# A setup generator in a stream of its own, its rotation tables last and queued behind the decay masks, and a recurrence with two working steps per chunk

## The chip, the cores and the metric

The kernel runs on one core of a Trainium2 chip. The metric is device time in microseconds (us) for one execution, the median of three runs. The engines are called by the profile's names: PE (TensorE matmul; PEld its weight loads), DVE (VectorE), ACT (ScalarE), POOL (GpSimd), SP (SyncE, which here only issues DMAs).

## The reference, cut to what matters

One layer of a decoder trunk over 2048 rows of width 1024: a mixer, cross-attention into 256 memory rows, and a gated MLP. The change lies in the mixer, which has two groups of heads side by side:

```
proj = rmsnorm(x) @ w_in
y_s5  = s5_mixer(proj[:, :256], lam, dt, b, c, ...)          # diagonal group
y_ssd = ssd_mixer(z, xbc, dt_raw, conv_w, a_log, ...)        # 12 heads, chunks of 128 rows
x = x + concat([y_s5, y_ssd]) @ w_out

# s5: h[l] = a * h[l-1] + (B u[l]), a complex, 64 states in each of 16 groups; y = Re(C h) + d*u
# ssd, per chunk c and head h:
#   lmat = exp(where(causal, acs[l] - acs[s], -inf));  cb = C_c B_c^T
#   y_diag = (cb * lmat) @ (x*dt);  y_off = (C_c @ prev) * exp(acs)
#   prev = prev * exp(acs_last) + B_c^T @ (decay * x * dt)
```

The parameters of the diagonal group are turned into matrices that don't depend on the rows: `ww` (input to state), `cct` (state to output, and the direct term) and `tab`, cosines and sines of the phase at 256 positions for each of 16 groups (the rotation tables).

## The kernel before, in words

The mixer's input projection is done by `MixerIn.run`: four blocks of 512 rows, in each 22 projections of 128 columns. One projection is 24 matmuls of 128x512 in two halves of 12 (L123 to L125, the three products of a split of each operand into a high and a low part, L98 and L99). After each half `Kit.step()` takes one step of each of two lists of generators, so that their instructions lie between the matmuls of the projections:

- `fg`: `ssd`, the recurrence over the four chunks of a block, for one half (`pr`) of the heads at a time. It runs during the next ten or twelve projections. Its parts for a chunk are `stage_in` (transposes of x and B, L415 and L421), `stage_cb` (the product C B^T at L430, times the decays at L434), `stage_y` (L443 to L458) and `stage_out` (L466 to L470). The decays themselves are `fetch_L`, on POOL's queue: a DMA that spreads a row of `acs` over 128 partitions (L387) and an `affine_select` that masks it (L388), then six exponentials on ACT (`decay`, L403). The rows of `acs` come from `dtprep`: a copy on DVE (L371), then a DMA on POOL's queue (L372).
- `bg`: `norm1_rest`, which normalizes the rows of the later blocks (sum of squares on ACT, L136; the scale on DVE, L130; the power -0.5 on POOL, L131; the product on DVE, L139; transposes on PE, L148), 60 steps long, and behind it `s5_setup`. Short generators are put ahead of these as they arise: `ssq`, and `mem.prep()`, the norm of the memory rows, in the last block.

`s5_setup` is 112 steps long: small DVE instructions (sine and cosine, powers), then the rotation tables on POOL (40 steps: eight of small products, L639 to L644, and two per group of three 128x256 instructions each, L654 to L660, with a DMA to DRAM per group, L661), then for each quarter of the groups four combinations of three 128x512 DVE instructions each (L725 to L727), with matmuls (L743, L744), transposes (L768) and DMAs on POOL's queue (L731). The tables are made in the SBUF tiles `b1`, `b2`, `Ca`, `Cb` and `Ba`, into which the later part loads its parameters (L705, on SP's queue) and writes its results.

There are two steps per projection and one at the start of each later block. What is left of `bg` when the projections are done is drained in one go (`k.drain(bg=True)`), ahead of the key and value projections of the cross-attention, `mem.proj`.

The order on each engine's queue isn't that of the program text. It is fixed when the kernel is built, by the framework's scheduler: the program order gives each instruction its priority, and on an engine that its own cost model sees idle the scheduler issues the first by priority whose inputs it takes to be ready. So instructions that are written late can run early: the first memsets of the tables (L633), written at about the 65th step, start at 0.95 us. On the chip each queue then runs strictly in this order, whether the inputs are late or not.

Of the kernel before, what the change touches and what calls it, by code (L numbers as in the profile page):

```python
# [9 lines left out]
F32 = mybir.dt.float32  # L10
# [3 lines left out]
ALU = mybir.AluOpType  # L14
AX = mybir.AxisListType
P = 128
# [8 lines left out]
def bcol(a, n):  # L25

    return a.rearrange("p (a b) -> p a b", b=1).to_broadcast([a.shape[0], a.shape[1], n])


class Kit:  # L30


    def __init__(self, tc, cx):
        self.tc, self.nc = tc, tc.nc
        self.V, self.S, self.G, self.TE = tc.nc.vector, tc.nc.scalar, tc.nc.gpsimd, tc.nc.tensor
        ep = cx.enter_context
        self.cp = ep(tc.tile_pool(name="const", bufs=1))
        self.dp = ep(tc.tile_pool(name="dram", bufs=1, space=bass.MemoryType.DRAM))
        self.pp = ep(tc.tile_pool(name="ps", bufs=8, space=bass.MemoryType.PSUM))
        self.sm = ep(tc.tile_pool(name="small", bufs=4))  # L40
        self.fg, self.bg = [], []
        nc = self.nc
        self.ident = self.cp.tile([P, P], F32, name="ident")
        make_identity(nc, self.ident)
        self.m05 = self.cp.tile([P, 1], F32, name="m05")
        nc.vector.memset(self.m05, -0.5)
        self.gains = self.cp.tile([P, 32], F32, name="gains")
# [26 lines left out]


    def step(self, n=1, m=1):
        for lst, k in ((self.fg, n), (self.bg, m)):
            for _ in range(k):
                while lst:
                    try:  # L80
                        next(lst[0])
                        break
                    except StopIteration:
                        lst.pop(0)

    def drain(self, bg=False):
        lst = self.bg if bg else self.fg
        while lst:
            try:
                next(lst[0])  # L90
            except StopIteration:
                lst.pop(0)


    def halves(self, src, hi, lo, scale=None):
# [78 lines left out]
class MixerIn:  # L174
# [208 lines left out]
    def fetch_L(self, b, pr, c):  # L383

        L = self.Ls[:, self.nL % 4]
        self.nL += 1
        self.k.G.dma_start(out=L.rearrange("p h l -> p (h l)"), in_=flat(self.d["acs"][b, c:c + 1, pr * 6:pr * 6 + 6, :]).partition_broadcast(P))  # L387
        self.k.G.affine_select(out=L, in_=L, pattern=[[0, 6], [1, P]], compare_op=ALU.is_ge, fill=-1e30, base=0, channel_multiplier=-1)  # L388
        self.L[b, pr, c] = L

    def ssd(self, b, pr, dd, xs, Bs, Cs, zs, sqacc):
# [69 lines left out]
        def stage_out(c):  # L461
# [5 lines left out]
            for i in range(3):  # L467
                j = pr * 3 + i
                V.scalar_tensor_tensor(gt[i][:, cs], xs[i][:, cs], self.D[:, j:j + 1], py[:, i * 128:i * 128 + 128], op0=ALU.mult, op1=ALU.add)
                V.tensor_tensor(gt[i][:, cs], gt[i][:, cs], zs[j][:, cs], op=ALU.mult)  # L470
        stage_in(0)
        yield
        for c in range(4):
            stage_cb(c)
            n = pr * 4 + c + 3
            if n < 8:
                self.fetch_L(b, n // 4, n % 4)
            if c < 3:
                decay(c + 1)
            yield  # L480
            if c < 3:
                stage_in(c + 1)
                yield
            stage_y(c)
            yield
            if c:
                stage_out(c - 1)
                yield
        stage_out(3)
        yield  # L490
        for i in range(3):
# [20 lines left out]
        k.rstd(self.d["rs"][:, b * 4:b * 4 + 4], pq[:, 0:4], 0.25 / 768, 1e-6)  # L512
        yield

    def run(self, last):
        k = self.k
        hs = self.hs
        k.bg.insert(0, self.norm1_rest())
        for b in range(self.NB):
            if b:  # L520
                with k.tc.high_priority(400):
                    hs = [k.split(*raw, tag="h") for raw in hraw]
                    hs += [k.split(*raw, tag="h") for raw in self.fetch_h(b, range(4, 8))]
                k.step(2)
            sqacc = self.zp.tile([P, 512], F32, tag="sqa", name="sqa", bufs=2)
            zs = [None] * 6
            dtp = self.dtprep(hs, b)
            for i in range(2):
                p = self.proj(hs, i)
                ut = k.t()  # L530
                k.S.activation(ut, p, AF.Copy)
                k.nc.scalar.dma_start(out=self.d["u"][i][:, b * 512:b * 512 + 512], in_=ut)
                next(dtp, None)
            for pr in range(2):
                for i in range(3):
                    if b == self.NB - 1 and pr == 0 and i == 2:
                        k.bg.insert(0, last)
                    zs[pr * 3 + i] = self.zgate(self.proj(hs, 2 + pr * 3 + i), pr * 3 + i)
                    next(dtp, None)
                xs = []  # L540
                for i in range(3):
                    xs.append(self.conv(self.proj(hs, 8 + pr * 3 + i), pr * 3 + i))
                    next(dtp, None)
                Bs, Cs = [], []
                for i in range(2):
                    Bs.append(self.conv(self.proj(hs, 14 + pr * 2 + i), 6 + pr * 2 + i))
                    if pr == 1 and i == 1 and b + 1 < self.NB:
                        hraw = self.fetch_h(b + 1, range(4))
                    Cs.append(self.conv(self.proj(hs, 18 + pr * 2 + i), 10 + pr * 2 + i))
                k.drain()  # L550
                k.fg.append(self.ssd(b, pr, self.dd, xs, Bs, Cs, zs, sqacc))


def s5_setup(k, a, d, up, NJ):
# [71 lines left out]
        if q % 4 == 3:  # L626
            yield
    yield
    tw = sp.tile([P, 16, 8], F32, tag="tw", name="tw")
    few = []  # L630
    for n, q0 in (("B", 3), ("A", 7)):
        fc, fs = (sp.tile([P, 16, 16], F32, tag="5" + x, name="f" + x) for x in (("b1", "b2") if n == "B" else ("Ca", "Cb")))
        G.memset(fc[:, :, 0:1], 1.0)  # L633
        G.memset(fs[:, :, 0:1], 0.0)
        for q in range(4 if n == "B" else nst - 4):
            m = 1 << q
            er, ei, t = bcol(Er[:, q0 + q, :], m), bcol(Ei[:, q0 + q, :], m), tw[:, :, 0:m]
            co, so, ci, si = fc[:, :, m:2 * m], fs[:, :, m:2 * m], fc[:, :, 0:m], fs[:, :, 0:m]
            G.tensor_tensor(co, ci, er, op=ALU.mult)  # L639
            G.tensor_tensor(t, si, ei, op=ALU.mult)  # L640
            G.tensor_tensor(co, co, t, op=ALU.subtract)
            G.tensor_tensor(so, ci, ei, op=ALU.mult)
            G.tensor_tensor(t, si, er, op=ALU.mult)
            G.tensor_tensor(so, so, t, op=ALU.add)  # L644
            yield
        few.append((fc, fs))
    (cb, sb), (ca, sa) = few
    na = NJ // 16
    for g in range(16):
        tab = sp.tile([P, 2, na, 16], F32, tag="tab", name="tab", bufs=2)  # L650
        wk = sp.tile([P, 16, 16], F32, tag="5Ba", name="wk")[:, 0:na]
        a_ = lambda v: v[:, g, 0:na].rearrange("p (a b) -> p a b", b=1).to_broadcast([P, na, 16])
        b_ = lambda v: v[:, g, :].rearrange("p (a b) -> p a b", a=1).to_broadcast([P, na, 16])
        G.tensor_tensor(tab[:, 0], a_(ca), b_(cb), op=ALU.mult)  # L654
        G.tensor_tensor(wk, a_(sa), b_(sb), op=ALU.mult)
        G.tensor_tensor(tab[:, 0], tab[:, 0], wk, op=ALU.subtract)
        yield
        G.tensor_tensor(tab[:, 1], a_(sa), b_(cb), op=ALU.mult)
        G.tensor_tensor(wk, a_(ca), b_(sb), op=ALU.mult)
        G.tensor_tensor(tab[:, 1], tab[:, 1], wk, op=ALU.add)  # L660
        G.dma_start(out=d["tab"][g], in_=tab.rearrange("p h a b -> p h (a b)"))  # L661
        yield

    Xr, Xi, Yr, Yi = (sp.tile([P, 16, 9], F32, tag=n, name=n) for n in ("Xr", "Xi", "Yr", "Yi"))
    V.memset(Xr[:, :, 0:1], 1.0)
# [66 lines left out]
    for q in range(4):  # L732
# [26 lines left out]
        for w in range(2):  # L759
            if w == 0:  # L760
                WT = comb(gs, Ba, Yr[:, gs, 0:8], Bb, Yi[:, gs, 0:8], ALU.add)
            else:
                WT = comb(gs, Ba, Yi[:, gs, 0:8], Bb, Yr[:, gs, 0:8], ALU.subtract)
            for _ in range(4):
                yield
            p = k.ps()
            for i in range(4):
                TE.transpose(p[:, i * 128:i * 128 + 128], WT[:, i * 128:i * 128 + 128], k.ident)  # L768
            Ws = k.t()
            S.activation(Ws, p, AF.Copy)  # L770
            put(d["ww"][gs, :, w * 128:w * 128 + 128], Ws)
            yield


def stage_s5(k, a, d, T):
# [748 lines left out]
def trunk(tc, a, out, T):  # L1524
    with ExitStack() as cx:
# [8 lines left out]
        with ExitStack() as c1:  # L1534
            k.open(c1, 3, r=8, w=8, h=16, t=25)
            mem = Memory(k, a, d)
            with ExitStack() as c2:
                d["s5p"] = c2.enter_context(tc.tile_pool(name="s5p", bufs=1))
                mix = MixerIn(k, c2, a, d, T)
                k.bg.append(s5_setup(k, a, d, mix.u, NJ))  # L1540
                mix.run(mem.prep())
                k.drain(bg=True)
                K, Vt = mem.proj("wk", "wv"), mem.proj("wv", None)
                k.drain()
                k.drain(bg=True)
# [51 lines left out]
```

## Time and profile before

| | us |
|---|---|
| median of 3 runs | 2741.43 (2739.88 to 2743.27) |
| the profiled execution, its own time | 2741.57 |
| its span, first to last instruction | 2739.9 |
| PE busy | 2625.9 (96%) |
| DVE busy | 2136.0 (78%) |
| ACT busy | 1324.6 (48%) |
| POOL busy | 482.3 (18%) |
| mean granted PE clock | 0.983 |

The mixer's projections fill the span from about 15 to 728 us. In the profile's lists a group of instructions has its line, engine, operation, output tile and input tiles, and its count; then busy time and the mean duration in ns. In a list of waits, "PE ps L148 <- DVE raw L139" says that PE's instruction of line 148 that writes `ps` stood waiting for DVE's instruction of line 139 that writes `raw`; then come total us, times, and the longest. A row of stretches gives for each engine the busy time and the count in that stretch, then the granted PE clock, the busy share of the DMA engines and GB/s. In a timeline, the time in brackets is how long the engine was idle just before, and what ended it.

### The profile page before, as it was taken

How to read it: one execution, taken by the hardware profiler on the slowest of the kernel's cores; microseconds unless marked ns; L12 is line 12 of the kernel's file. 1: busy time of each engine (PE TensorE's matmuls, PEld its weight loads, DVE VectorE, ACT ScalarE, POOL GpSimd, SP SyncE). 2: the span in 40 equal slices, each digit the busy share in tenths (PEclk: the TensorE clock that was granted, in tenths of full speed). 3: DMA queues.
4: the chain of work that ended last, by engine and by line, in shares of the span. 5: the costliest groups of instructions: out<-in, count | busy, mean ns of one | idle time of the engine just before them, and what ended most of it. 6: DMA issues, size and time to landing. Idle time of an engine off the chain costs nothing. (4 is left out here: it accounts for less than half of the span.)

```text
span 2739.9 us, 38565 instructions
## 1 busy us (share of the span) xinstructions
PE 2625.9 (96%) x12636; PEld 2187.3 (80%) x12636; DVE 2136.0 (78%) x4015; ACT 1324.6 (48%) x2657; POOL 482.3 (18%) x807
## 2 busy tenths in 40 slices
PE   8479999999799999999999999999999999999997
PEld 6367888878699788888888888887888888788876
DVE  8568888888877654878789788879887887677776
ACT  4345654446445412778745454435444344433333
POOL 3840101101103110110311222212111111000000
PEclk9789999999899999999999999999999999999999
DMA  5445443344368783546665433425222227887886
GB/s 171 131 145 176 151 129 112 110 137 141 106 201 293 259 290 141 184 162 231 215 219 174 127 112 120 131 89 177 93 85 78 92 63 255 280 295 237 257 263 203
DMA packets 241538, 468.24 MB, mean 171 GB/s; under 512 B 30008, under 2 KB 72056, under 8 KB 241336
## 3 DMA queue, kind: packets, MB, share of 16 engines
q1 hardware_dynamic: 182312, 341.38, 38.1%
q0 software_dynamic: 30416, 105.50, 11.9%
q10 hardware_dynamic: 28608, 18.88, 2.2%
q8 instruction: 100, 1.64, 0.2%
q14 instruction: 102, 0.84, 0.1%
HBM read 350.67 MB, written 114.39 MB: 170 GB/s over the span
## 5 line engine op out<-in xcount | busy, mean ns | idle before, releaser
L124 PE MATMUL ps<-H,W 128*128 128x512 f32 x952 | 370.6, 389 | 0.5 <-DVE H L99 0.5
L123 PE MATMUL ps<-H,W 128*128 128x512 f32 x952 | 370.9, 390 | 0.0
L125 PE MATMUL ps<-H,W 128*128 128x512 f32 x952 | 370.5, 389 | 0.1
L123 PE MATMUL ps<-h,w 128*128 128x512 f32 (+1 forms) x736 | 301.8, 410 | 13.4 <-ACT w L98 10.5
L125 PE MATMUL ps<-h,w 128*128 128x512 f32 (+1 forms) x736 | 288.9, 392 | 0.5 <-DVE w L99 0.5
L124 PE MATMUL ps<-h,w 128*128 128x512 f32 (+1 forms) x736 | 287.6, 391 | 0.7 <-DVE h L102 0.7
L123 PE MATMUL ps<-Q,A 128*128 128x512 f32 x704 | 275.9, 392 | 1.0 <-ACT A L98 0.8
L125 PE MATMUL ps<-Q,A 128*128 128x512 f32 x704 | 274.5, 390 | 0.0
L124 PE MATMUL ps<-Q,A 128*128 128x512 f32 x704 | 273.9, 389 | 0.0
L98 ACT ACTIVATE W<-S 128x512 fp32r<-128x512 f32 x191 | 118.9, 630 | 283.2 <-DVE S L1350 143.5
L98 ACT ACTIVATE w<-r 128x512 fp32r<-128x512 f32 x224 | 139.1, 627 | 187.9 <-PE ps L124 143.6
L124 PEld LDWEIGHTS ps<-H,W 128*128 128x128 f32 x952 | 178.7, 188 | 38.2 <-DVE H L99 1.5
L125 PEld LDWEIGHTS ps<-H,W 128*128 128x128 f32 x952 | 178.7, 188 | 37.6 <-DVE W L99 0.5
L123 PEld LDWEIGHTS ps<-H,W 128*128 128x128 f32 x952 | 178.7, 188 | 37.4 <-ACT H L98 0.4
L99 DVE TENSOR_TENSOR w<-r,w 128x512 fp32r<-128x512 f32 x224 | 159.8, 717 | 62.2 <-ACT w L98 59.1
L123 PEld LDWEIGHTS ps<-h,w 128*128 128x128 f32 x736 | 140.8, 191 | 38.8 <-ACT w L98 10.9
L125 PEld LDWEIGHTS ps<-h,w 128*128 128x128 f32 x736 | 140.1, 190 | 31.3 <-DVE w L99 1.6
L124 PEld LDWEIGHTS ps<-h,w 128*128 128x128 f32 x736 | 141.0, 192 | 27.0 <-DVE h L102 2.1
L125 PEld LDWEIGHTS ps<-Q,A 128*128 128x128 f32 x704 | 132.1, 188 | 28.7 <-DVE A L99 1.1
L123 PEld LDWEIGHTS ps<-Q,A 128*128 128x128 f32 x704 | 132.2, 188 | 28.2 <-ACT A L98 1.0
L124 PEld LDWEIGHTS ps<-Q,A 128*128 128x128 f32 x704 | 132.3, 188 | 26.8
L98 ACT ACTIVATE A<-F 128x512 fp32r<-128x512 f32 (+1 forms) x146 | 89.0, 631 | 123.4 <-PE ps L124 63.9
(489 smaller groups left out, 6299.6 us busy)
## 6 DMA issues: line engine op xcount, KB each, us to landing
A<-actd SPq DMA_DIRECT2D x192, 256.0 KB, 3.9
r<-in_w_in SPq DMA_DIRECT2D x176, 256.0 KB, 2.9
R<-in_w_up SPq DMA_DIRECT2D x176, 256.0 KB, 2.9
R<-in_w_down SPq DMA_DIRECT2D x132, 256.0 KB, 4.3
actd<-U POOLq DMA_DIRECT2D x88, 256.0 KB, 3.1
A<-actd SPq DMA_DIRECT2D x96, 192.0 KB, 3.8
R<-h3Cd SPq DMA_DIRECT2D x56, 256.0 KB, 3.6
L<-acsd POOLq DMA_DIRECT2D x32, 384.0 KB, 4.3
```

The lines of the kernel that those rows point to most:

```text
L98: self.S.activation(hi, src, AF.Copy)
L99: self.V.tensor_tensor(lo, src, hi.bitcast(F32), op=ALU.subtract)
L123: self.TE.matmul(out, lh, rh, start=first and i == 0, stop=False)
L124: self.TE.matmul(out, lh, rl, start=False, stop=False)
L125: self.TE.matmul(out, ll, rh, start=False, stop=last and i == n - 1)
```

## The change

1. `s5_setup` leaves `bg` and becomes the only generator of a third list, `xg`, of which `step` also takes one step each time. It is put there at the start of the second half (`pr == 1`) of the first block, at the 25th step, while `norm1_rest` is still running in `bg`.
2. The rotation tables move from the middle of `s5_setup` to its end, after the last quarter. They take 56 steps there in place of 40 (an empty step in each group).
3. The first table instructions of each piece are traced under `behind()`, which orders them on POOL's queue after `k.mark`, the most recently traced mask (L388). The rest of a piece follows them by its data.
4. In `ssd`, `stage_in`, `stage_cb`, the next mask and the next decays are one step (`head`), with `stage_out` of the chunk before; `stage_y` is another; two empty steps lie between. The generator has 20 steps in place of 18.

```
     def step(self, n=1, m=1):
-        for lst, k in ((self.fg, n), (self.bg, m)):
+        for lst, k in ((self.fg, n), (self.bg, m), (self.xg, m)):
...
+    def behind(self):
+        return self.tc.issue_after(self.mark.ins)
...
-        self.k.G.affine_select(out=L, in_=L, ...)
+        self.k.mark = self.k.G.affine_select(out=L, in_=L, ...)
...
-        stage_in(0)
-        yield
-        for c in range(4):
+        def head(c):
+            stage_in(c)
             stage_cb(c)
             n = pr * 4 + c + 3
             if n < 8:
                 self.fetch_L(b, n // 4, n % 4)
             if c < 3:
                 decay(c + 1)
+        head(0)
+        yield
+        for c in range(4):
+            yield
+            stage_y(c)
+            yield
             yield
             if c < 3:
-                stage_in(c + 1)
-                yield
-            stage_y(c)
-            yield
+                head(c + 1)
             if c:
                 stage_out(c - 1)
-                yield
+            yield
...
             for pr in range(2):
+                if b == 0 and pr == 1:
+                    k.xg.append(beside)
...
     # s5_setup: the tables, from after the sines and cosines to after the last quarter
+        with k.behind():
+            G.memset(fc[:, :, 0:1], 1.0)
+            G.memset(fs[:, :, 0:1], 0.0)
...
     for g in range(16):
...
+        with k.behind():
+            G.tensor_tensor(tab[:, 0], a_(ca), b_(cb), op=ALU.mult)
+            G.tensor_tensor(wk, a_(sa), b_(sb), op=ALU.mult)
         G.tensor_tensor(tab[:, 0], tab[:, 0], wk, op=ALU.subtract)
         yield
+        yield
+        with k.behind():
+            G.tensor_tensor(tab[:, 1], a_(sa), b_(cb), op=ALU.mult)
         G.tensor_tensor(wk, a_(ca), b_(sb), op=ALU.mult)
         G.tensor_tensor(tab[:, 1], tab[:, 1], wk, op=ALU.add)
         G.dma_start(out=d["tab"][g], in_=tab.rearrange("p h a b -> p h (a b)"))
         yield
...
-                k.bg.append(s5_setup(k, a, d, mix.u, NJ))
-                mix.run(mem.prep())
+                mix.run(mem.prep(), s5_setup(k, a, d, mix.u, NJ))
                 k.drain(bg=True)
```

More of the change, by code (lines that the diff above doesn't have):

```diff
@@ L40, in __init__ @@
         self.sm = ep(tc.tile_pool(name="small", bufs=4))
-        self.fg, self.bg = [], []
+        self.fg, self.bg, self.xg, self.mark = [], [], [], None
         nc = self.nc
@@ L86, in drain @@
     def drain(self, bg=False):
[L87 to L92, printed above, removed]
+        for lst in (self.bg, self.xg) if bg else (self.fg,):
+            while lst:
+                try:
+                    next(lst[0])
+                except StopIteration:
+                    lst.pop(0)
+    def behind(self):
+        return self.tc.issue_after(self.mark.ins)
     def halves(self, src, hi, lo, scale=None):
@@ L387, in fetch_L @@
         self.k.G.dma_start(out=L.rearrange("p h l -> p (h l)"), in_=flat(self.d["acs"][b, c:c + 1, pr * 6:pr * 6 + 6, :]).partition_broadcast(P))
-        self.k.G.affine_select(out=L, in_=L, pattern=[[0, 6], [1, P]], compare_op=ALU.is_ge, fill=-1e30, base=0, channel_multiplier=-1)
+        self.k.mark = self.k.G.affine_select(out=L, in_=L, pattern=[[0, 6], [1, P]], compare_op=ALU.is_ge, fill=-1e30, base=0, channel_multiplier=-1)
         self.L[b, pr, c] = L
@@ L513, in ssq, with run @@
         yield
-    def run(self, last):
+    def run(self, last, beside):
         k = self.k
@@ L628, in s5_setup @@
     yield
[L629 to L662, printed above, removed]
     Xr, Xi, Yr, Yi = (sp.tile([P, 16, 9], F32, tag=n, name=n) for n in ("Xr", "Xi", "Yr", "Yi"))
@@ L772, in s5_setup @@
             yield
+    tw = sp.tile([P, 16, 8], F32, tag="tw", name="tw")
+    few = []
+    for n, q0 in (("B", 3), ("A", 7)):
+        fc, fs = (sp.tile([P, 16, 16], F32, tag="5" + x, name="f" + x) for x in (("b1", "b2") if n == "B" else ("Ca", "Cb")))
+        with k.behind():
+            G.memset(fc[:, :, 0:1], 1.0)
+            G.memset(fs[:, :, 0:1], 0.0)
+        for q in range(4 if n == "B" else nst - 4):
+            m = 1 << q
+            er, ei, t = bcol(Er[:, q0 + q, :], m), bcol(Ei[:, q0 + q, :], m), tw[:, :, 0:m]
+            co, so, ci, si = fc[:, :, m:2 * m], fs[:, :, m:2 * m], fc[:, :, 0:m], fs[:, :, 0:m]
+            G.tensor_tensor(co, ci, er, op=ALU.mult)
+            G.tensor_tensor(t, si, ei, op=ALU.mult)
+            G.tensor_tensor(co, co, t, op=ALU.subtract)
+            G.tensor_tensor(so, ci, ei, op=ALU.mult)
+            G.tensor_tensor(t, si, er, op=ALU.mult)
+            G.tensor_tensor(so, so, t, op=ALU.add)
+            yield
+        few.append((fc, fs))
+    (cb, sb), (ca, sa) = few
+    na = NJ // 16
+    for g in range(16):
+        tab = sp.tile([P, 2, na, 16], F32, tag="tab", name="tab", bufs=2)
+        wk = sp.tile([P, 16, 16], F32, tag="5Ba", name="wk")[:, 0:na]
+        a_ = lambda v: v[:, g, 0:na].rearrange("p (a b) -> p a b", b=1).to_broadcast([P, na, 16])
+        b_ = lambda v: v[:, g, :].rearrange("p (a b) -> p a b", a=1).to_broadcast([P, na, 16])
+        with k.behind():
+            G.tensor_tensor(tab[:, 0], a_(ca), b_(cb), op=ALU.mult)
+            G.tensor_tensor(wk, a_(sa), b_(sb), op=ALU.mult)
+        G.tensor_tensor(tab[:, 0], tab[:, 0], wk, op=ALU.subtract)
+        yield
+        yield
+        with k.behind():
+            G.tensor_tensor(tab[:, 1], a_(sa), b_(cb), op=ALU.mult)
+        G.tensor_tensor(wk, a_(ca), b_(sb), op=ALU.mult)
+        G.tensor_tensor(tab[:, 1], tab[:, 1], wk, op=ALU.add)
+        G.dma_start(out=d["tab"][g], in_=tab.rearrange("p h a b -> p h (a b)"))
+        yield
 def stage_s5(k, a, d, T):
```

## The prediction

> **What bounds the kernel now.** I read the page first, then the busy time of each engine in stretches, then the waits of PE and of what PE waited for, then single rows of the timeline.
>
> ```profile
> PE 2625.9 (96%) x12636; PEld 2187.3 (80%) x12636; DVE 2136.0 (78%) x4015; ACT 1324.6 (48%) x2657; POOL 482.3 (18%) x807
> ```
>
> PE is busy for 96% of the span. Only where PE stands still, or runs at a lower clock, is there time to win without taking work away, and the stretches show where that is:
>
> ```profile
> core 0: us, PE busy (x) PEld busy (x) DVE busy (x) ACT busy (x) POOL busy (x), PEclk, DMA share, GB/s
> 50.00:72.00 22.00, 21.95 (x104) 17.68 (x103) 19.43 (x68) 8.23 (x17) 20.44 (x43) 1.00 0.33 106
> 72.00:166.00 94.00, 41.85 (x156) 32.66 (x155) 50.57 (x57) 30.24 (x67) 84.46 (x115) 0.69 0.38 122
> 728.00:741.00 13.00, 0.78 (x4) 0.42 (x3) 10.41 (x20) 5.75 (x10) 0.76 (x1) 0.63 0.45 136
> 741.00:750.00 9.00, 8.25 (x46) 7.85 (x45) 3.04 (x7) 3.00 (x6) 1.50 (x2) 0.58 0.30 89
> 750.00:760.00 10.00, 10.00 (x86) 10.00 (x85) 8.33 (x17) 3.35 (x7) 0.00 (x0) 1.00 0.35 105
> ```
>
> The columns after the stretch are its length, then PE, PEld, DVE, ACT and POOL. From 50 to 72 us PE issues 104 matmuls in 21.95 us, 0.211 us each. From 72 to 166 us it issues 156 in 94 us. At the pace before they would take 156 x 0.211 = 32.9 us, so this stretch loses 61.1 us. POOL is busy in it for 84.46 of 94 us, nearly all of that rotation tables. From 728 to 750 us PE issues 4 + 46 = 50 in 22 us; at the pace of 750 to 760 (86 in 10 us, 0.116 each) they would take 5.8 us, so 16.2 us are lost there.
>
> Why PE stands in the first stretch, by the waits of PE, of DVE and of ACT from 60 to 200 us:
>
> ```profile
> PE ps L148 <- DVE raw L139: 25.0, 2, 19.1
> PE ps L430 <- DVE t L316: 16.1, 1, 16.1
> PE ps L123 <- ACT w L98: 10.5, 1, 10.5
> ```
>
> ```profile
> DVE raw L139 <- POOL ss L131: 32.0, 4, 13.2
> ```
>
> ```profile
> ACT L L403 <- POOL L L388: 22.4, 3, 12.8
> ```
>
> PE's waits sum to 25.0 + 16.1 + 10.5 = 51.6 us; the other 9.5 of the 61.1 us are matmuls at a low clock after each gap (0.69 on average in the stretch). All lead back to POOL's queue. DVE stood 32.0 us for the power that `norm1_rest` takes on POOL, and while it stood no weight was split and no convolution done. ACT stood 22.4 us for decay masks. The delay of the first mask can be followed:
>
> ```profile
> 63.12 0.28 DVE L371 COPY rows<-ps 48x128 f32<-48x128 f32 x1
> ```
>
> ```profile
> 73.60 0.54 POOL L372 DMA_DIRECT2D acsd<-rows  x1
> ```
>
> ```profile
> 83.15 0.69 ACT L403 ACTIVATE L<-L,nacs 128x128 f32<-128x128 f32 x2 [12.79 <-POOL L L388]
> ```
>
> The rows of `acs` are ready at 63.12 + 0.28 = 63.4 us. POOL, in the midst of tables, comes to their DMA at 73.60, 10.2 us late, and ACT, which had come to the exponentials first, waits 12.79 us, with the splits of the weights behind them. PE's 10.5 us are that wait. SP has one such wait:
>
> ```profile
> SPq L705 <- POOL tab L658: 16.9, 1, 16.9
> ```
>
> That is the load of the parameters into tiles that the tables still use, with the loads of the weights behind it in SP's queue.
>
> The second loss is at the end of the mixer:
>
> ```profile
> 740.61 1.09 PE L768 MATMUL ps<-ident,t 128*128 128x128 f32 x4 [12.22 <-DVE t L727]
> ```
>
> PE's transposes for the last quarter of `s5_setup` (L768) wait 12.22 us for its combinations, which stand on DVE behind the last convolutions. They are in PE's queue because `bg` has 60 + 112 steps and some 17 of `ssq` and `mem.prep`, and the mixer only 44 + 3 x 45 = 179: ten are left, which are drained ahead of `mem.proj`.
>
> **The change part by part.** The sum is made against the profiled execution's own time, 2741.6 us, which is 0.1 above the median of the runs.
>
> *The tables leave the first blocks.* The stretch of 61.1 us has no other cause that I can find, so it goes, but not wholly: what is late next is the chain of block 0 itself. The rows of `acs` are ready at 63.4 and the mask follows by two DMAs, so ACT may still come to the exponentials a little early. I leave 6 us, the smaller of the two gaps on L148 (25.0 - 19.1 = 5.9); the bounds are 0 and 25 (both gaps). Gain 61.1 - 6 = 55.1. The parameter loads (L705) no longer wait for tables, which is in that sum.
>
> *The setup starts at the 25th step.* It needs 128 steps and one call to end, and from there the mixer has 20 + 3 x 45 = 155. So nothing of it is left at the drain, and the ten steps that block PE's queue are gone. What is late next is the split of the first weights of `mem.proj`, on DVE:
>
> ```profile
> 731.27 0.68 DVE L99 TENSOR_TENSOR w<-r,w 128x512 fp32r<-128x512 f32 x1
> ```
>
> This split ends at 731.95 us, some 3 us after the projections, and part of the DVE work ahead of it is combinations that go. I leave 3 us of the 16.2; bounds 0 and 4. Gain 13.2. The same combinations, transposes and DMAs on POOL's and SP's queues are issued per step as before, only some 36 steps earlier; I cost them at nothing, since they lay beside projections before, where DVE has the slack counted next.
>
> *The tables come back later.* By the steps they lie from step 97 to step 152, from early in block 2 to the middle of block 3. The copy of the rows of `acs` gives the length of a block:
>
> ```profile
> L371 DVE COPY rows<-ps x4: 269/274/275, 63.1 to 615.5; 48x128 f32<-48x128 f32 x4
> ```
>
> (615.5 - 63.1 - 61.1) / 3 = 164 us for 45 steps, 3.6 us a step, so 56 steps are 204 us. How much POOL works there, with a mask beside it for scale:
>
> ```profile
> L388 POOL TENSOR_SCALAR_AFFINE_SELECT L<-L 128x768 f32<-128x768 f32 x32 | 30.8, 967 | 72.8 <-DMA L<-acsd 72.6
> ...
> L660 POOL TENSOR_TENSOR tab<-tab,wk 128x256 f32<-128x256 f32 x16 | 14.8, 923 | 1.1
> ...
> L656 POOL TENSOR_TENSOR tab<-tab,wk 128x256 f32<-128x256 f32 x16 | 12.0, 748 | 0.1
> ```
>
> There are six groups of sixteen, costliest and cheapest shown: 6 x (14.8 + 12.0) / 2 = 80 us of POOL in 204. POOL has the room. But DVE slows beside them. The same DVE work, first between 64 and 167 us, then between 200 and 700:
>
> ```profile
> L313 DVE SCALAR_TENSOR_TENSOR t<-t,cw 128x512 f32<-128x512 f32 x21 | 23.1, 1101 | 0.4
> L99 DVE TENSOR_TENSOR w<-r,w 128x512 fp32r<-128x512 f32 x16 | 16.9, 1057 | 10.5 <-ACT w L98 10.5
> ...
> L417 DVE TENSOR_TENSOR u<-ps,dt 128x384 f32<-128x384 f32 x1 | 0.5, 544 | 0.0
> ```
>
> ```profile
> L313 DVE SCALAR_TENSOR_TENSOR t<-t,cw 128x512 f32<-128x512 f32 x126 | 95.1, 755 | 7.5 <-ACT t L311 6.1 <-issue 0.3
> L99 DVE TENSOR_TENSOR w<-r,w 128x512 fp32r<-128x512 f32 x133 | 91.9, 692 | 38.3 <-ACT w L98 35.5 <-PE ps L430 1.0 <-ACT u L423 0.8
> ...
> L417 DVE TENSOR_TENSOR u<-ps,dt 128x384 f32<-128x384 f32 x24 | 13.2, 552 | 3.4 <-PE ps L415 3.4
> ```
>
> L313 takes 1101 in place of 755 ns, L99 1057 in place of 692: 1.49 times as long. So 80 us of tables can cost DVE at most 80 x (1 - 1/1.49) = 26 us. How full is DVE in blocks 2 and 3?
>
> ```profile
> 530.00:560.00 30.00, 27.93 (x141) 22.73 (x139) 26.93 (x60) 18.35 (x39) 2.64 (x4) 1.00 0.38 118
> 560.00:590.00 30.00, 29.00 (x162) 22.97 (x162) 27.51 (x65) 14.17 (x26) 2.80 (x4) 1.00 0.58 182
> 590.00:620.00 30.00, 30.00 (x171) 26.09 (x171) 24.75 (x75) 11.09 (x24) 2.93 (x5) 1.00 0.26 83
> 650.00:680.00 30.00, 30.00 (x162) 24.78 (x162) 27.45 (x53) 14.37 (x30) 5.60 (x8) 1.00 0.40 127
> ```
>
> ```profile
> L727 DVE TENSOR_TENSOR t<-t 128x512 f32<-128x512 f32 x16 | 11.0, 687 | 0.0
> ```
>
> DVE is busy for (26.93 + 27.51 + 24.75 + 27.45) / 4 = 26.7 of 30 us, 89%. In it are the sixteen combinations of three instructions, 3 x 11.0 = 33 us between 490 and 742 us, 13%, which will be done by then. That leaves 76%, and 26 us in 204 add 13%: 89% again. At that load PE stood 2.07 + 1.00 = 3.07 us in these 120, so I take 3.07 x 204 / 120 = 5 us. Bounds: 0 if DVE's slack takes it all, 26 if none. In these rows the tables cost 5; by the following they would cost less.
>
> The Trainium skill (GPSIMD Engine Reference, Key points) says that GpSimd shares its SBUF interfaces with VectorE and contends with VectorE instructions that have two SBUF inputs or run in a two-port mode. The trace bears that out: L417, which reads PSUM, takes 544 beside 552 ns, L313 and L99 half as long again. By that rule the recurrence's products with PSUM (L417's 13.2 us is one of seven such groups) would not slow; by my estimate from that the tables would cost about 3 us and the sum be 2676.
>
> *The waits of the tables on the mask.* A table piece now waits in POOL's queue for a mask, and behind it stand the next mask's DMA, the powers of `mem.prep` and `ssq`, and the DMAs of the setup; for these ACT (exponentials) and DVE (L139) wait. Nothing in this trace shows tables beside masks of block 2. From below it is 0, since the mask that a piece waits for is already issued; from above it is the gap of 10.5 us for each late mask (a rival, below). I take 0, because a piece is three instructions of about 0.8 us and a mask comes every 45 / 8 = 5.6 steps, 20 us.
>
> *Two working steps per chunk.* The same instructions; decays are issued four steps ahead of their use in place of one, C B^T in `ssd`'s second step in place of its third. What waits PE has on the recurrence in steady state:
>
> ```profile
> PE ps L457 <- DVE u L434: 0.9, 3, 0.4
> ```
>
> So it can give 0.9 us. It can cost PE one step's early start for each of eight runs, 12 x 0.211 = 2.5 us each, 20 in all, if the last convolution isn't done. I take 0, by the row.
>
> Sum: 2741.6 - 55.1 - 13.2 + 5 = 2678.3.
>
> **The rivals.** *The stall goes along with the tables.* DVE in blocks 2 and 3 turns out to be the bound beside them, the whole 26 us come onto the path, and one mask is late as at 73.60. For it speaks that DVE is fuller there than in block 0; against it that the pieces are spread over 204 us. 2678.3 - 5 + 26 + 10.5 = 2710.
>
> *The change doesn't do what it says.* The gaps from 72 to 166 us come back without tables, because `norm1_rest` and the masks of block 0 are late by themselves. Then only the end is won: 2741.6 - 13.2 = 2728. Against it: POOL is busy throughout the gaps.
>
> *Slower: the masks queue behind the tables.* ACT's queue is in order, so a mask behind a table piece holds up the weight splits. Some ten masks fall into the 56 steps. If each costs what the first one did, 10 x 10.5 = 105 us come to 2678.3 - 5: 2778. It is slower than before from the seventh such mask on (68 us are won without the 5). Against it: ACT's exponentials are now wanted four steps after they are issued, and POOL is free for more than half of that time.
>
> **How the numbers follow.** The forecast has a chance of 0.71, the first rival 0.18, the second 0.06, the slower one 0.05. The forecast's own range is 2660 to 2700: below, both losses wholly gone (2741.6 - 61.1 - 16.2 = 2664) and some luck with the recurrence; above, another 21 us by DVE or by a gap in block 0. The range that should hold 8 times in 10 is 2658 to 2716 and takes in the first rival. A measurement of this kernel can tell about 0.2%, 5.5 us. Faster has 0.92: forecast and both rivals that still win, less 0.03 for a mixture that comes out even; slower 0.05.
>
> **What the profile after would show.** Right: POOL without tables before about 330 us; from 72 to 110 us PE without gaps over 6 us and at full clock; the last transposes of the setup (L768's successor) well before the end of the mixer and no gap over 4 us there; DVE's L313 and L99 lengthened somewhere between 330 and 560 us. Wrong: PE waits on L148 or on ACT's splits in blocks 2 and 3; ACT waiting over 10 us for a mask there; PE gaps in block 0 that end with DVE or ACT while POOL is idle.

## The result and the profile after

| | median, us | lowest to highest | runs |
|---|---|---|---|
| before | 2740.55 | 2738.03 to 2743.27 | 6 |
| after | 2757.03 | 2751.27 to 2763.22 | 6 |

After / before is 1.0061 (95% interval 1.0042 to 1.0080). The change makes the kernel 16.5 us slower, where the prediction had it 63 us faster (2741 to 2678). 2757.0 lies above the whole predicted range. The miss is 79 us.

The first row is of the page of the kernel after: busy time, share of the span and count of each engine.

```profile
PE 2645.7 (96%) x12636; PEld 2199.3 (80%) x12636; DVE 2152.6 (78%) x4015; ACT 1326.6 (48%) x2657; POOL 495.9 (18%) x807
```

PE issues the same 12636 matmuls, but is busy for 2645.7 us where it was busy for 2625.9. DVE and POOL are busy 16.6 and 13.6 us longer, with as many instructions as before. The profiled execution took 2759.75 us, 2.7 above the median.

The stretches of the kernel after have the columns of the prediction's table; those that follow them are of the kernel before, at four of the same places.

```profile
72.00:166.00 94.00, 89.07 (x463) 75.13 (x462) 74.08 (x150) 55.98 (x120) 13.45 (x20) 0.96 0.50 159
...
300.00:400.00 100.00, 84.46 (x411) 69.10 (x410) 86.36 (x167) 48.15 (x95) 37.84 (x68) 0.85 0.39 124
400.00:500.00 100.00, 91.46 (x442) 75.49 (x441) 78.40 (x158) 42.04 (x87) 36.42 (x46) 0.94 0.31 104
460.00:480.00 20.00, 11.46 (x50) 8.76 (x48) 19.93 (x28) 10.14 (x24) 18.87 (x23) 0.90 0.37 119
500.00:600.00 100.00, 82.48 (x383) 65.85 (x382) 85.35 (x138) 43.29 (x88) 61.20 (x75) 0.86 0.38 126
600.00:700.00 100.00, 95.88 (x476) 78.93 (x474) 74.07 (x178) 47.50 (x104) 16.21 (x20) 0.97 0.29 98
750.00:775.00 25.00, 22.83 (x150) 20.27 (x149) 23.31 (x53) 14.98 (x28) 0.00 (x0) 1.00 0.30 95
```

```profile
300.00:400.00 100.00, 99.95 (x503) 84.15 (x502) 84.38 (x178) 64.97 (x133) 9.74 (x12) 1.00 0.42 130
400.00:500.00 100.00, 99.82 (x519) 82.65 (x518) 84.23 (x197) 49.42 (x102) 11.02 (x14) 1.00 0.36 119
500.00:600.00 100.00, 96.93 (x522) 80.28 (x521) 87.53 (x207) 48.15 (x99) 11.91 (x15) 1.00 0.43 136
600.00:700.00 100.00, 100.00 (x536) 85.06 (x535) 86.79 (x186) 57.64 (x130) 16.38 (x22) 1.00 0.38 123
```

The predicted gain is there. From 72 to 166 us PE issues 463 matmuls where it issued 156, and POOL is busy for 13.45 us in place of 84.46. From 750 us on PE is at work again at full clock. But between 300 and 700 us PE issues 411 + 442 + 383 + 476 = 1712 matmuls, at a clock down to 0.85. The kernel before issued 503 + 519 + 522 + 536 = 2080 at full clock. At its pace (400 us / 2080 = 0.192 us) 368 matmuls are 71 us. The row from 460 to 480 us is one of the places, with DVE busy throughout. So one loss was taken away and another one put in, later in the mixer.

PE stands there for these waits, from 200 to 740 us (total us, times, longest):

```profile
PE ps L434 <- DVE t L320: 12.5, 5, 4.7
PE ps L517 <- DVE sqa L504: 10.2, 2, 6.1
PE ps L425 <- DVE t L320: 6.4, 3, 2.6
PE ps L453 <- ACT u L427: 5.8, 2, 5.3
```

In the kernel before PE's longest wait on the recurrence in that part was 0.4 us (L457, shown in the prediction). Now it stands for the last step of a convolution (L320, which was L316: up to the new steps all lines are 4 later than before), for the copy of B on ACT (L427, was L423) and for the sum of the squares of the finished rows (L504). The waits behind the tables are gone from the first block. From 60 to 200 us, first DVE's row, then ACT's:

```profile
DVE raw L143 <- POOL ss L135: 3.2, 4, 1.1
```

```profile
ACT L L407 <- POOL L L392: 11.5, 4, 5.4
```

32.0 us have become 3.2, and 22.4 have become 11.5.

How far the mixer has come can be read from one instruction, the copy of the rows of `acs`, whose fourth start is in the last block:

```profile
L375 DVE COPY rows<-ps x4: 272/274/275, 59.6 to 645.8; 48x128 f32<-48x128 f32 x4
```

It starts the first block at 59.6 us in place of 63.1, and the last one at 645.8 in place of 615.5. That start is used as a mark below.

### The profile page after: what moved, and what is told of

It is laid out like the page before. It is cut to its first block, busy times and chain, and to the rows that moved or that the text cites. A ratio compares the mean times of both kernels' runs of the same rounds, so it can differ in the third digit from the quotient of the medians.

```text
span 2757.3 us, 38540 instructions
## 1 busy us (share of the span) xinstructions
PE 2645.7 (96%) x12636; PEld 2199.3 (80%) x12636; DVE 2152.6 (78%) x4015; ACT 1326.6 (48%) x2657; POOL 495.9 (18%) x807
## 5 line engine op out<-in xcount | busy, mean ns | idle before, releaser
L103 DVE TENSOR_TENSOR w<-r,w 128x512 fp32r<-128x512 f32 x224 | 164.6, 738 | 76.4 <-ACT w L102 75.4
L129 PEld LDWEIGHTS ps<-Q,A 128*128 128x128 f32 x704 | 132.1, 188 | 28.6 <-DVE A L103 0.8
```

The source lines that it names most:

```text
L103: self.V.tensor_tensor(lo, src, hi.bitcast(F32), op=ALU.subtract)
L129: self.TE.matmul(out, ll, rh, start=False, stop=last and i == n - 1)
```

## The experiments

Each kernel was timed beside runs of the kernel before on the same chip (medians 2739.8 to 2741.1 us). Two theories stood at first. **S**: the loss is in the steps of the recurrence. **T**: it is in the tables, which now run on POOL beside a DVE that is nearly full.

**The kernel after with the old steps.** `ssd` alone goes back to four steps per chunk.

```
-        head(0)
+        stage_in(0)
         yield
         for c in range(4):
+            stage_cb(c)
...
+                decay(c + 1)
             yield
+            if c < 3:
+                stage_in(c + 1)
+                yield
             stage_y(c)
             yield
-            yield
-            if c < 3:
-                head(c + 1)
             if c:
                 stage_out(c - 1)
-            yield
+                yield
```

> The changed kernel with the recurrence's old four steps per chunk. Theory S (the new steps put the first C B^T of each run in PE's queue before the last convolution is done): the waits on that product in the blocks without tables go, 18 us of gaps and some 7 us of low clock, and part of those beside the tables; about 2725 us. Theory T (only the tables cost, by slowing DVE in fuller blocks): no change, 2757 us.

Measured: 2718.2 us, ratio to before 0.9930 (0.9915 to 0.9945). The new steps cost 2757.0 - 2718.2 = 38.9 us beside the other edits, and without them the rest of the change is a gain. The mark says the same:

```profile
L375 DVE COPY rows<-ps x4: 273/275/276, 59.5 to 609.8; 48x128 f32<-48x128 f32 x4
```

The last block starts 36.0 us earlier than with the new steps (609.8 against 645.8).

**The new steps alone, on the kernel before.** The diff's edit of `ssd` and nothing else:

```
-        stage_in(0)
-        yield
-        for c in range(4):
+        def head(c):
+            stage_in(c)
             stage_cb(c)
...
+        head(0)
+        yield
+        for c in range(4):
             yield
-            if c < 3:
-                stage_in(c + 1)
-                yield
             stage_y(c)
...
```

> The kernel before with the recurrence's new steps and nothing else. Theory S: slower than before by about 25 us, 2766 us, with waits of 3 to 5 us on the first C B^T of most of the eight runs. Theory T: within 5 us of before.

Measured: 2785.3 us, ratio 1.0170 (1.0155 to 1.0186), 45 us slower; more than S had put down. So the steps need no table beside them to do harm. PE's waits in this kernel from 190 to 740 us:

```profile
PE ps L449 <- ACT u L423: 14.7, 3, 5.7
PE ps L430 <- DVE t L316: 11.0, 5, 3.4
PE ps L421 <- DVE t L316: 4.0, 3, 1.5
```

```profile
L371 DVE COPY rows<-ps x4: 273/276/276, 63.4 to 652.7; 48x128 f32<-48x128 f32 x4
```

They come three to five times each, and 652.7 - 615.5 = 37.2 us are lost by the start of the last block. Three blocks begin in this part. One such start, first rows of PE and of ACT in this kernel, then stretches of 10 us in this kernel and in the kernel before:

```profile
238.16 0.33 PE L421 MATMUL ps<-ident,t 128*128 128x128 f32 x1 [1.44 <-DVE t L316]
...
243.56 1.65 PE L449 MATMUL ps<-u 128*128 128x192 f32 x4 [4.28 <-ACT u L423]
247.32 0.80 PE L430 MATMUL ps<-t 128*128 128x128 f32 x2 [2.11 <-DVE t L316]
```

```profile
240.81 0.71 ACT L501 ACTIVATE t<-t,nw 128x512 f32<-128x512 f32 x1
...
243.12 0.38 ACT L423 ACTIVATE u<-ps 128x256 f32<-128x256 f32 x1 [0.93 <-DMA h1T<-raw]
```

```profile
235.00:245.00 10.00, 4.28 (x17) 2.98 (x15) 9.25 (x21) 7.49 (x15) 0.00 (x0) 0.74 0.93 314
245.00:255.00 10.00, 7.88 (x29) 5.07 (x29) 5.17 (x11) 1.58 (x4) 0.55 (x1) 0.58 0.24 83
```

```profile
235.00:245.00 10.00, 9.83 (x46) 6.38 (x47) 9.44 (x18) 7.79 (x16) 0.00 (x0) 1.00 0.98 308
245.00:255.00 10.00, 10.00 (x59) 8.38 (x59) 7.60 (x15) 3.98 (x8) 0.55 (x1) 1.00 0.62 177
```

At the start of a later block two steps are taken ahead of its first projection. With the old steps they issue the decays and `stage_in(0)`; now they issue the decays and `head(0)`, with C B^T in it, and the first `stage_y` (L443 to L458) follows in the fourth step in place of the fifth. The last work of the block before is not done by then, and PE's order on its queue is fixed. In this trace the recurrence's L421, L443, L449 and L430 come in PE's queue with hardly a matmul of a projection among them. L421 waits for the last convolution. L449 takes B from ACT's copy (L423), and on ACT that copy is behind the splits of the rows and the squares and scales of the block before (L499, L501; the rows of ACT show the last of these, then L423 at 243.12). L430 waits for a further convolution. While one of them waits, nothing behind it on PE's queue can run. From 235 to 255 us PE issues 17 + 29 = 46 matmuls where the kernel before issues 46 + 59 = 105, and the clock falls to 0.74 and 0.58. 59 matmuls at 0.192 us are 11 us. The other two starts show the same chain, here by its longest wait:

```profile
419.31 1.65 PE L449 MATMUL ps<-u 128*128 128x192 f32 x4 [5.71 <-ACT u L423]
597.39 1.65 PE L449 MATMUL ps<-u 128*128 128x192 f32 x4 [4.74 <-ACT u L423]
```

All of the waits on L449 and L421 in the list above lie at the three starts. PE issues 44 matmuls from 408 to 428 us and 42 from 588 to 608, where the pace of 0.192 us would give 104. With the first start that makes about 35 us of the 37.2.

**The first head one step later, on the kernel with the new steps alone.**

```
+        yield
         head(0)
...
             yield
             stage_y(c)
             yield
-            yield
+            if c < 3:
+                yield
```

> The kernel before with the new steps, but the first head (transposes and C B^T of chunk 0) one step later, so that a half projection lies between it and the end of the last convolution. Theory S1 (the cost of the new steps is that the first C B^T of a run comes before the last convolution is done): most of the 45 us go, 2750 us or less. Rival S2 (the lumped steps cost by themselves, in all chunks): 2775 us or more.

Measured: 2751.9 us, ratio 1.0038 (1.0027 to 1.0049): 33 of the 45 us are back. The two working steps per chunk stay; one empty step is put ahead of them, and one is dropped ahead of the last chunk's `stage_out`. PE's waits and the mark:

```profile
PE ps L421 <- DVE t L316: 3.4, 2, 1.9
PE ps L430 <- DVE t L316: 2.9, 1, 2.9
```

```profile
L371 DVE COPY rows<-ps x4: 273/278/283, 63.0 to 624.6; 48x128 f32<-48x128 f32 x4
```

L449 is gone from the list, L421 and L430 are 6.3 us in place of 15.0, and the mark stands at 624.6 in place of 652.7. The empty step puts the first C B^T and the first `stage_y` of each run back to the third and the fifth step, where the old order had them. So it is where the chunks of a run lie that costs (by the waits, the first one, against the first projections of a block), and not the two steps per chunk as such. 11 us over the kernel before are left; the runs don't settle whether these are what is left of L421 and L430 or the later `stage_out`.

**The tables left out, in three kernels.** T's part was measured by leaving out the six products per group; a memset stands in their place.

```
-        G.tensor_tensor(tab[:, 0], a_(ca), b_(cb), op=ALU.mult)
...
-        G.tensor_tensor(tab[:, 1], tab[:, 1], wk, op=ALU.add)
+        G.memset(tab, 0.5)
```

In the kernel after:

> The changed kernel without the six products of each group of the rotation tables (a constant is written in their place, so the diagonal group's output is wrong; all DMAs and steps stay). Theory S: the tables cost what the prediction allowed, 5 to 26 us, so 2731 to 2752 us. Theory T: all that was lost against the prediction is here, so about 2680 us.

In the kernel before:

> The kernel before without the same products (a constant in their place). If the first loss of the prediction is the tables', 61 us less a rest of 6: 2686 us. If block 0 is late by itself, over 2720 us.

In the kernel after with old steps:

> The changed kernel with the old steps and without the six products of each group (a constant in their place). If the tables in their new place cost the rest that the first run (2718 us) lacks to the forecast: 2680 us. If the setup's early start, or a rest in block 0, costs it: 2700 us or more.

Measured:

| | with products | without | the products cost |
|---|---|---|---|
| after | 2757.0 | 2730.1 (ratio to before 0.9967, 0.9957 to 0.9977) | 26.9 |
| before | 2740.3 | 2690.9 (0.9828, 0.9813 to 0.9843) | 49.4 |
| after, old steps | 2718.2 | 2688.7 (0.9804, 0.9789 to 0.9819) | 29.5 |

So the first place of the tables did cost the kernel before about 50 us, and the second place still costs 27 to 30.

The last column is rather too small. The memsets and the DMAs that are left need no inputs, and in these kernels all sixteen memsets start between 1 and 46 us: in the kernel after with old steps and without products POOL is busy for 8.6 and 10.6 us in the first two stretches of 20 us, with products for 3.4 and 1.1. DVE's longest wait for a power behind them is 3.0 to 7.4 us, and the copy of the rows in the first block is 7.5, 10.2 and 9.4 us late. From that first copy to the last one the products cost 31.8, 56.7 and 33.6 us. What the new steps cost is much the same without products: 2730.1 - 2688.7 = 41.4 us.

The stretches show where the products cost, first the kernel after with old steps, then the same without products:

```profile
400.00:500.00 100.00, 90.06 (x427) 75.38 (x427) 79.29 (x129) 44.78 (x99) 50.47 (x67) 0.93 0.35 114
500.00:600.00 100.00, 89.65 (x426) 72.19 (x424) 83.80 (x175) 40.63 (x77) 43.53 (x54) 0.91 0.37 117
```

```profile
400.00:500.00 100.00, 99.37 (x509) 84.54 (x507) 78.41 (x171) 50.92 (x110) 12.65 (x16) 1.00 0.34 112
500.00:600.00 100.00, 98.83 (x511) 80.90 (x510) 80.73 (x201) 50.09 (x104) 7.50 (x12) 0.98 0.37 118
```

```profile
L375 DVE COPY rows<-ps x4: 273/275/277, 68.9 to 585.6; 48x128 f32<-48x128 f32 x4
```

Between 400 and 600 us PE issues 853 matmuls with the products and 1020 without: 167, at 0.192 us 32 us. The mark moves from 609.8 to 585.6, 24.2 us, though the first block starts 9.4 us later. With the products the clock is 0.93 and 0.91: PE was busy for only 90 of 100 us, in many short gaps.

Two reasons were possible: **C**, products on POOL slow DVE's own instructions, and **F**, DVE and what hangs on it are so full there that the tables cost whichever engine makes them. The groups of DVE in the kernel after from 456 to 490 us, when POOL has tables, their DMAs and three masks, speak for C:

```profile
L103 DVE TENSOR_TENSOR w<-r,w 128x512 fp32r<-128x512 f32 x8 | 9.5, 1182 | 0.0
L320 DVE SCALAR_TENSOR_TENSOR t<-t 128x512 f32<-128x512 f32 x3 | 8.3, 2778 | 2.0 <-ACT t L319 2.0
L317 DVE SCALAR_TENSOR_TENSOR t<-t,cw 128x512 f32<-128x512 f32 x9 | 8.0, 888 | 0.1
...
L311 DVE COPY t<-halo 128x3 f32<-128x3 f32 x2 | 2.5, 1264 | 0.0
...
L473 DVE SCALAR_TENSOR_TENSOR t<-t,D,ps 128x128 f32<-128x128 f32 x6 | 1.9, 335 | 0.0
```

A split (L103) takes 1182 ns where the quiet part of the kernel before took 692 (its L99), a convolution's multiply-add (L317) 888 against 755. The 2778 of its last step (L320) are a mean of 1.11, 0.67 and one of 6.55 us, with the first of POOL's rows beside it:

```profile
456.22 6.55 DVE L320 SCALAR_TENSOR_TENSOR t<-t 128x512 f32<-128x512 f32 x1 [2.01 <-ACT t L319]
```

```profile
456.28 0.63 POOL L775 TENSOR_TENSOR tab<-fCa,fb 128x256 f32<-128x256 f32 x1
```

From 456.28 to 462.0 us POOL runs eight products and a mask without a gap, the products in 0.61 to 0.73 us each, and this one DVE instruction ends only behind them, at 462.8. In the kernel after with old steps two DVE products (L474) take 7.26 us from 422.79 on, beside the same run of POOL (423.55 to 429.3). So a part of DVE's busy time is time in which it is held up. PE has no wait for these three L320; in this stretch it stands 2.4 us for L103 and longest for the sum of the squares, which DVE makes among the slowed rows:

```profile
478.48 1.84 PE L517 MATMUL ps<-one,sqa 128*128 128x1 f32 x8 [6.12 <-DVE sqa L504]
```

L473, which reads PSUM, is not slower (335 ns; 336 from 360 to 390 us). A copy of three elements (L311) takes 1264.

**The products on DVE.** The kernel after with old steps, with the six products per group issued on VectorE and so not behind a mask:

```
-        with k.behind():
-            G.tensor_tensor(tab[:, 0], a_(ca), b_(cb), op=ALU.mult)
+        V.tensor_tensor(tab[:, 0], a_(ca), b_(cb), op=ALU.mult)
...
-        G.tensor_tensor(tab[:, 1], tab[:, 1], wk, op=ALU.add)
+        V.tensor_tensor(tab[:, 1], tab[:, 1], wk, op=ALU.add)
```

> The changed kernel with the old steps, and with the six products of each group on DVE in place of POOL, not queued behind a mask. Theory C (what costs is that DVE's and POOL's instructions slow each other, which the order of the queues does not allow for): 2690 to 2705 us, though DVE has 30 us more to do. Rival F (DVE is too full in blocks 2 and 3, whoever takes its time): 2718 us or more.

Measured: 2689.6 us, ratio 0.9815 (0.9795 to 0.9834). It is 28.6 us faster than with the same products on POOL, and within 1 us of no products at all (which is flattered by the late start there). DVE does more work and the kernel is faster: F is refuted as the main cause. From the first copy of the rows to the last, 57.7 to 582.4 us, the products on DVE cost 8.0 us, those on POOL 33.6, so F can hold at most 8 of them. Nor is it masks that come late in POOL's queue: from 200 to 740 us ACT stands 39.1 us for masks with the products on POOL, 31.7 with them on DVE, and 39.0 in the kernel before. The same product on POOL (kernel after with old steps) and on DVE (this one):

```profile
L773 POOL TENSOR_TENSOR tab<-fCa,fb 128x256 f32<-128x256 f32 x16 | 12.6, 787 | 0.2
```

```profile
L772 DVE TENSOR_TENSOR tab<-fCa,fb 128x256 f32<-128x256 f32 x16 | 6.7, 417 | 7.0 <-POOL fCa L759 6.7 <-DMA tabd<-tab 0.3
```

On average 787 ns on POOL (the shortest 611), 417 on DVE; all six groups together are 80.5 us on POOL and 40.9 on DVE.

**All tables on DVE.** The small products and memsets too:

```
-        with k.behind():
-            G.memset(fc[:, :, 0:1], 1.0)
+        V.memset(fc[:, :, 0:1], 1.0)
...
-            G.tensor_tensor(co, ci, er, op=ALU.mult)
+            V.tensor_tensor(co, ci, er, op=ALU.mult)
```

> The changed kernel with the old steps and all of the tables on DVE, the small products too. Theory C (POOL's and DVE's instructions slow each other): the one large gap that is left with the products on DVE, 7.4 us on DVE's splits beside the small products on POOL, goes, with its low clock: about 2680 us. Rival F (DVE too full): 2690 us or more.

Measured: 2681.8 us, ratio 0.9783 (0.9763 to 0.9804), another 8 us by medians, though the two intervals overlap.

**The products on DVE in the kernel before.** The six products per group, and nothing else:

```
-        G.tensor_tensor(tab[:, 0], a_(ca), b_(cb), op=ALU.mult)
+        V.tensor_tensor(tab[:, 0], a_(ca), b_(cb), op=ALU.mult)
...
-        G.tensor_tensor(tab[:, 1], tab[:, 1], wk, op=ALU.add)
+        V.tensor_tensor(tab[:, 1], tab[:, 1], wk, op=ALU.add)
```

> The kernel before with the six products of each group on DVE in place of POOL, and nothing else. Theory C: the first loss goes where it is, without moving the tables; as without the products (2691 us) plus DVE's time where it doesn't fit, 2691 to 2705 us. Rival P (the tables lie in the wrong place, early, whichever engine makes them): over 2715 us.

Measured: 2695.0 us, ratio 0.9830 (0.9815 to 0.9846). One engine's name per line brings 45 us without any of the change: most of what the tables cost in their first place came from POOL, as the prediction had read it, and not from their early place as such.

**The stream alone.** The kernel before with only `xg`: the setup from the 25th step, tables still in its middle and not queued, old steps.

```
-                k.bg.append(s5_setup(k, a, d, mix.u, NJ))
-                mix.run(mem.prep())
+                mix.run(mem.prep(), s5_setup(k, a, d, mix.u, NJ))
...
+                if b == 0 and pr == 1:
+                    k.xg.append(beside)
```

> The kernel before with the setup in its own stream from the 25th step and nothing else: tables in the middle of the setup, not queued behind masks, old steps. If the end of the mixer is the setup's drain: 13 to 16 us less than before, 2726 us, with the gaps from 72 to 166 us as they were. If the tables move along with the start of the setup: the gaps shift and shrink, under 2715 us.

Measured: 2732.2 us, ratio 0.9963 (0.9949 to 0.9976), a gain of 10 us (6.6 to 14.0) by the ratio. The early gaps stay as they were; PE's longest and the stretch:

```profile
132.09 1.09 PE L148 MATMUL ps<-ident,raw 128*128 128x128 f32 x4 [19.17 <-DVE raw L139]
```

```profile
72.00:166.00 94.00, 40.66 (x152) 31.80 (x151) 50.33 (x57) 29.93 (x66) 84.44 (x116) 0.70 0.37 121
```

19.17 us against 19.11, 152 matmuls against 156. The gain is at the end of the mixer: the wait of 12.22 us on the last combination is gone. Against it stands a new wait of 3.7 us at 407 us, of PE's L334 for a copy of the setup on ACT (L772 of this kernel).

**No queueing behind the masks.** The kernel after with old steps, without `behind()`:

```
-        with k.behind():
+        if True:
```

> The changed kernel with the old steps and the tables not queued behind masks. Theory C: what costs is the time that tables run beside a full DVE, which stays the same; within 10 us of the same kernel with the queue order (2718 us). Rival Q (the order behind the masks bunches the tables, or is what protects the masks): more than 15 us away, either way.

Measured: 2734.1 us, ratio 0.9973 (0.9963 to 0.9984), 15.9 us slower than with it by medians, some 12 by the ratios. The expectation that it wouldn't matter by more than 10 us failed. ACT's wait for masks, from 200 to 740 us, in this kernel and then in the one that queues the tables:

```profile
ACT L L407 <- POOL L L392: 74.3, 15, 37.0
```

```profile
ACT L L407 <- POOL L L392: 39.1, 15, 6.4
```

Unqueued, ACT stands 37.0 us for one mask, with the splits of the weights behind it, and PE in turn 29.4:

```profile
PE ps L127 <- ACT w L102: 29.4, 1, 29.4
```

Queued, ACT's longest such wait is 6.4 us. So `behind()` does what its name says. It also closes a gap in the reading of the products on DVE, which lost their place in POOL's queue together with POOL: without that place, but on POOL, they cost more and not less.

**The stream alone with all tables on DVE.** Tables in the middle of the setup, unqueued, old steps; small products, memsets and the six products per group on VectorE:

```
-        G.memset(fc[:, :, 0:1], 1.0)
+        V.memset(fc[:, :, 0:1], 1.0)
...
-        G.tensor_tensor(tab[:, 0], a_(ca), b_(cb), op=ALU.mult)
+        V.tensor_tensor(tab[:, 0], a_(ca), b_(cb), op=ALU.mult)
...
```

> The setup in its own stream from the 25th step, tables in the middle of it as before, all of them on DVE, old steps. Theory C: the place hardly matters once POOL is out of it, 2675 to 2690 us. Rival P: tables in the middle cost more than tables last, over 2700 us.

Measured: 2680.9 us, ratio 0.9775 (0.9749 to 0.9802). It is even with the kernel whose tables come last (2681.8). Off POOL, the tables' place no longer matters to within what these runs tell. Both are some 58 us faster than the kernel before and 75 us faster than the change; they are the fastest versions measured.

## Why the prediction was wrong, step by step

| step of the sum | forecast | measured | from |
|---|---|---|---|
| tables leave the first blocks | -55.1 | -49.4 (by the ratio -47, -43 to -51); -56.7 from the first copy to the last | before, without products |
| setup starts at the 25th step | -13.2 | -8.9 (by the ratio -10, -6.6 to -14) | stream alone |
| tables come back later | +5 (0 to 26) | +29.5; +33.6 from the first copy to the last | after with old steps, with and without products |
| waits of tables on masks | 0 | 15.9 less than tables that don't wait | after with old steps, unqueued |
| two working steps | 0 (-0.9 to 20) | +38.9 beside the rest, +41.4 without products, +45 alone | old steps; no products; steps alone |

The miss of 79 us is 38.9 for the steps, 24.5 for the tables' return (29.5 - 5), and 15.4 for the rest (2688.7 without products and with old steps, where the sum without its last terms was 2673.3). Most of the 15.4 is in the kernel that it was measured with: without products its first block starts 9.4 us later than with them (68.9 against 59.5). An estimate, if that passes on to the end in full: 6 us are left for the rest, 4.3 of them in the second row, and the tables' return costs some 39 us in place of 29.5.

**The step that failed is "Two working steps per chunk".** The prediction priced it at 0 "by the row": PE's waits on the recurrence were 0.9 us in steady state. That row was true of the old order only. It says that the inputs of the recurrence were on time where they were asked for, and the change moves where they are asked for. How early each input was there was not read; at a block's start the margin was less than the step that the change takes away. The upper bound named the right condition ("if the last convolution isn't done"), but priced it at 12 matmuls for each of eight runs, as if only the projections of one step were lost. What is lost is all of PE's queue until a convolution, ACT's copy of B and a further convolution have come, one after the other, at the three block starts: 11 to 12 us at each, with the lower clock in it.

**The size of "The tables come back later"** was the second miss, and its mechanism was right. The rows show the longer durations beside POOL again, and more than the 1.49 taken (1182 against 692 is 1.7, and one instruction took 6.55 us). Two readings made it small. The 80 us of tables were spread over 204 us, at a mean load of 89%, and they came in bursts. In the kernel after most pieces run from 456 to 488 us and from 508 to 584, and in a burst DVE has no slack at all (from 460 to 480 us it is busy, or held up, for 19.93 of 20, and PE issues 50 matmuls). And the bound of 26 us counted DVE's time only: the gaps of PE cost clock as well, so that the price came out above the bound. The rival that had the whole 26 us on the path came to 2710, near the 2718.2 of the kernel with old steps.

The rule of the Trainium skill (GPSIMD Engine Reference, Key points), that the contention is with DVE instructions of two SBUF inputs, agrees with L103 and L317 against L473. The copy L311 has one input and is longer too; whether it ran in a two-port mode, which the rule names beside the two inputs, no row here shows. What the prediction worked out from it, a cost of 3 us, fell with the spreading.

**The gains.** Both were where the prediction read them: POOL's queue in the first block (32.0 us of DVE's wait have become 3.2) and the last combinations at the end (10 us by the stream alone). The early one was about as large as forecast, 49.4 to 56.7 us against 55.1.

**The slower rival** had the sign right and the place wrong. Masks late behind tables do exist, 37.0 us for one, but only without `behind()`; the change has it. Among the signs that would show the forecast wrong were PE's waits on L148 and on ACT's splits, and none on the convolutions.

## What to carry to other kernels

A row of waits near zero says that an operand came in time where it is now asked for, and nothing about how much earlier it may be asked for. When a change merges steps, look up for each input of the moved instruction when it is ready at the worst place (here a block's start, with the last block's tail still on ACT), and price a miss by the whole of an in-order queue behind it. For side work, ask first which engine it slows and then where it goes: putting the tables' products on DVE, with no step moved, brought 45 us here, and moving them to a later place on POOL some 20 (49.4 - 29.5).

## What the runs showed of the hardware that was not expected

- Products of 128x256 take on average 1.9 times as long on POOL (787 ns, the shortest 611) as on DVE (417) and, while on POOL, lengthen DVE's instructions around them so far that 40.9 us more work on DVE made the kernel 28.6 us faster. The Trainium skill (GPSIMD Engine Reference, Engine selection) gives such two-input work to VectorE and GpSimd as about twice as slow; the means agree, and the second effect is the larger one here.
- A DVE copy of three elements per partition took 1264 ns beside POOL's products, as against 263 from 360 to 390 us beside small ones. One multiply-add of 128x512, 747 ns on average in that quiet stretch, took 6.55 us, as long as a run of nine POOL instructions without a gap beside it.
- Idle time in many short gaps went with a longer busy time than about as much of it in fewer, longer gaps. In the kernel after PE is idle for about as long as in the kernel before (2757.3 - 2645.7 = 111.6 us against 2739.9 - 2625.9 = 114.0), yet its busy time is 19.8 us longer for the same matmuls, with clocks of 0.85 to 0.94 in the stretches from 300 to 600 us. The gaps listed there are 6.1 us and shorter.
